# Four wide score products in a row, then four narrow corrections, in the recurrent layer of a two-layer backbone

## The chip, the cores and the metric

The kernel runs on one core of one Trainium2 chip. The metric is the device time of one execution in microseconds, as the median of several runs. All data is fp32 in DRAM; most matrix products split their operands into a rounded part and a remainder ("hi" and "lo") and add three products.

## The reference

A latent stream of 512 tokens by 1024 features and a context of 256 tokens pass through two layers. The first layer mixes the tokens with a bidirectional gated recurrence (8 heads of 128), the second with a short convolution; each is followed by a squared-ReLU MLP with 4096 hidden units. Norms are modulated by vectors from a conditioning input (adaLN). The part that matters here is one chunk of the recurrence, run for each head and direction:

```python
def step(s, blk):
    qb, kb, vb, gb = blk
    cum = jnp.cumsum(gb, axis=2)
    ref = cum[:, :, CHUNK // 2 - 1:CHUNK // 2]
    last = cum[:, :, -1:]
    o_inter = jnp.einsum('bhck,bhkv->bhcv', qb * jnp.exp(cum), s)
    scores = jnp.einsum('bhck,bhsk->bhcs', qb * jnp.exp(cum - ref), kb * jnp.exp(ref - cum))
    scores = jnp.where(lower, scores, 0.0)
    o_intra = jnp.einsum('bhcs,bhsv->bhcv', scores, vb)
    s_new = jnp.exp(last[:, :, 0, :, None]) * s + jnp.einsum(
        'bhsk,bhsv->bhkv', kb * jnp.exp(last - cum), vb)
    return s_new, o_inter + o_intra
```

Chunks are 64 tokens long. The output is the latent stream after a final norm.

## The kernel before

The program has three stretches: up to about 95 us the adaLN vectors, the norm and the first projections; from there to about 490 us the recurrent layer, head by head; behind it the MLPs and the convolution layer, which are long rows of 512-column products.

The recurrent layer works on pairs of heads. For each head TensorE makes the forget gates of the latent tokens (`ps_fl`) and of the context (`ps_fc`). ScalarE and VectorE turn them into logs, running sums and exponentials (`logs`, lines 646 to 712) and into scaled queries and keys (`latent_ops`, lines 740 to 761). Meanwhile TensorE makes the values (`psv`, even heads) or a gate projection (`ps_p`, odd heads). Then the recurrence of the head begins: `context_states` (line 714) transposes the context keys (`ctr`, written by VectorE at line 711) and makes the start states (`cst`), and `recurrence` (line 794) does both directions and the output.

The kernel takes two 64-token chunks together as one block of 128 tokens, so a head has four blocks `n`. In `scores` (line 763) a block's scores are one product of 128 by 128 (line 768, weights `kt`, moving `qt`). A 64 by 64 quarter of it, where queries of one chunk meet keys of the other, has the wrong scaling, and a second product from the sliced keys and queries `kl` and `ql` writes over that quarter (line 769). It lands on PSUM partitions 0 to 63 in the forward direction (`f` = 0) and 64 to 127 in the backward one. All four blocks of a direction lie in one PSUM tile `sc`; VectorE copies its unmasked entries out with one `copy_predicated` (line 772, `scm`).

Around it, for each direction, `states` (line 774) transposes scaled keys (`ktr`), which ScalarE copies (`kT`, line 781), makes the state products (`kv`, line 784) and lets VectorE update the states in three steps (`S`, line 789). When both directions are through, VectorE adds the two score tiles (`scs`, line 804) and TensorE makes the output `po` (lines 808 to 810; the third product of a block reads `scs`).

TensorE's order in a recurrence is written out by hand. Each of its instructions goes through `fill.step`, which chains it behind the last one, and `fill.gap` puts a number of product instructions of the next head (or of the output projection, `ps_woa`) in between; the numbers stand in the table `GAPS`. The PSUM tiles `ctr`, `cst`, `ktr`, `kv` and `sc` come from one pool of three buffers (`ps_sm`), so a new tile waits until VectorE or ScalarE has read an older one. VectorE's queue also holds the rounding remainders of weights (line 317) and sums for later adaLN vectors (`acc`, lines 442 and 444), which wait for their own DMAs.

Of the kernel before, what the change touches and what calls it, by code (L numbers as in the profile page):

```python
# [46 lines left out]
def dit_kernel(ctx, tc, x, c, ctx_in, c_ctx, ada_w, ada_b, norm1, norm2, norm_f, mlp_w1, mlp_w2,  # L47
# [28 lines left out]
    def sm_tile(name):  # L76
        return ps_sm.tile([P, 512], F32, tag="sm", name=name)
# [67 lines left out]
    for nm, ap in (("norm1", n1),  # L145
# [5 lines left out]
        n = ap.shape[0]  # L151
# [611 lines left out]
    def scores(o, d, hd, fill):  # L763
        ps = sm_tile(f"sc_{hd}_{d}")
        f = d
        for n in range(4):
            s = slice(n * P, (n + 1) * P)
            fill.step(nc.tensor.matmul(ps[:, s], lhsT=o["kt"][:, s], rhs=o["qt"][:, s], start=True, stop=True))  # L768
            fill.step(nc.tensor.matmul(ps[64 * f:64 * f + 64, n * P + 64 * (1 - f):n * P + 64 * (1 - f) + 64],
                                       lhsT=o["kl"][:, n * 64:n * 64 + 64], rhs=o["ql"][:, n * 64:n * 64 + 64],  # L770
                                       start=True, stop=True))
        nc.vector.copy_predicated(scm[d], pm[d], ps.rearrange("p (n t) -> p n t", t=P))
# [21 lines left out]
    def recurrence(hd, ops, s0, v, fill):  # L794

        S = []
        for d in range(2):
            S.append(states(ops[d], d, s0[d], v, f"{hd}_{d}", fill))
            if d:
                fill.gap()  # L800
            scores(ops[d], d, hd, fill)
# [457 lines left out]
```

## Time and profile before

| | before |
|---|---|
| median of 3 runs | 1429.88 us (1428.97 to 1430.18) |
| the profiled execution | 1430.36 us, its span 1428.6 us |
| TensorE, matmul | 1372.0 us busy, 96% |
| TensorE, weight loads | 1165.9 us busy, 82% |
| VectorE | 911.0 us, 64% |
| ScalarE | 578.6 us, 40% |
| mean granted TensorE clock | 0.990 |
| wide score products (line 768) | 128 instructions, first at 108.3, last at 476.8 us |
| corrections (line 769) | 128 instructions, first at 108.6, last at 477.1 us |

A busy TensorE is not TensorE at its peak: matmuls are pipelined, a recorded matmul is longer than its distance to the next one, and its end is modelled. The distance from start to start tells more. PE is the matmul row, PEld the weight load of the same instruction; 128\*64 is the part of the array that a matmul uses, rows by columns.

### The profile page before, as it was taken

The page shows a single profiled execution, that of the slowest core. Times are in us where ns is not written, and L with a number is a line of the kernel's source. Part 1 is how long each engine was busy: PE and PEld are TensorE (multiplying, and loading weights), DVE is VectorE, ACT ScalarE, POOL GpSimd, SP SyncE. Part 2 cuts the span into 40 slices and gives each one's busy share as a digit, 9 for nine tenths or more (in the row PEclk, how much of TensorE's full clock was granted, in tenths as well). Part 3 has the DMA queues.
Part 4 walks back from the last instruction along what each step waited for, and adds up shares of the span by engine and source line. Part 5 has one row for each costly group of instructions (what it writes and reads, how often), then busy time and mean ns, then how long its engine had stood idle before and what let it go on. Part 6 is the DMA issues. An engine that isn't in the chain of part 4 may idle for free.

```text
span 1428.6 us, 18668 instructions
## 1 busy us (share of the span) xinstructions
PE 1372.0 (96%) x7418; PEld 1165.9 (82%) x7418; DVE 911.0 (64%) x1378; ACT 578.6 (40%) x877; POOL 79.0 (6%) x87
## 2 busy tenths in 40 slices
PE   6999999999996989999999999999999999999997
PEld 4798887977885888888888889888889888888887
DVE  5695877878669598666576447544578544544536
ACT  6573447336435354133341433322244423142333
POOL 3000000000000121000000002000030100000000
PEclk9999999999998999999999999999999999999999
DMA  9713313423202235666555322332334533233311
GB/s 266 208 46 118 96 38 118 134 89 103 75 30 67 65 105 197 201 206 210 174 176 180 116 89 75 104 99 93 103 101 136 177 93 99 90 102 97 96 59 60
DMA packets 142267, 167.60 MB, mean 117 GB/s; under 512 B 6692, under 2 KB 121572, under 8 KB 142180
## 3 DMA queue, kind: packets, MB, share of 16 engines
q1 hardware_dynamic: 140964, 164.70, 36.4%
q0 software_dynamic: 1088, 1.65, 0.5%
q8 instruction: 58, 0.95, 0.3%
q14 instruction: 29, 0.24, 0.1%
q10 hardware_dynamic: 128, 0.05, 0.0%
HBM read 164.25 MB, written 2.14 MB: 116 GB/s over the span
## 4 chain that ended last, share of the span: by engine, by line
PE 74%; DVE 16%; DMA 3%; ACT 3%; issue 2%; SPq 0%; POOL 0%; DVEq 0%; ACTq 0%
PE ps_w L340 20%; PE ps_w L343 10%; PE ps_w2t L1197 4%; PE ps_w2t L1198 4%; PE ps_w2t L1196 4%; PE ps_fl L340 3%; DMA ada<-in_ada_w_dram 3%; PE ps_cvb L340 2%; PE ps_cwo L340 2%; PE ps_cvx L340 2%; PE ps_cvc L340 2%; PE ps_fl L343 2%; PE ps_fc L340 2%; PE sc L768 1%; PE ps_p L340 1%
## 5 line engine op out<-in xcount | busy, mean ns | idle before, releaser
L316 ACT CAST whi_w<-raw_w 128x1024 fp32r<-128x1024 f32 x128 | 134.0, 1051 | 277.0 <-PE ps_w L340 146.1
L317 DVE TENSOR_TENSOR wlo_w<-raw_w,whi_w 128x1024 fp32r<-128x1024 f32 x116 | 141.4, 1223 | 161.7 <-ACT whi_w L316 161.2
L340 PE MATMUL ps_w<-h_a_hi,whi_w 128*128 128x512 f32 (+1 forms) x576 | 207.6, 367 | 2.4 <-ACT h_a_hi L232 2.4
L340 PE MATMUL ps_w<-h_a_lo,whi_w 128*128 128x512 f32 x448 | 174.6, 390 | 0.0
L340 PEld LDWEIGHTS ps_w<-h_a_hi,whi_w 128*128 128x128 f32 x576 | 108.6, 189 | 21.1 <-ACT h_a_hi L232 2.8
L444 DVE SCALAR_TENSOR_TENSOR acc<-ada,cs,acc 128x1024 f32<-128x1024 f32 x70 | 89.8, 1282 | 50.8 <-DMA ada<-in_ada_w_dram 50.7
L343 PE MATMUL ps_w<-h_a_hi,wlo_w 128*128 128x512 f32 x448 | 119.8, 389 | 0.0
L1196 PE MATMUL ps_w2t<-whi_w,u_hi 128*128 128x512 f32 (+1 forms) x288 | 105.4, 366 | 0.0
L1197 PE MATMUL ps_w2t<-wlo_w,u_hi 128*128 128x512 f32 (+1 forms) x288 | 105.4, 366 | 0.0
L1198 PE MATMUL ps_w2t<-whi_w,u_lo 128*128 128x512 f32 (+1 forms) x288 | 105.4, 366 | 0.0
L340 PE MATMUL ps_w<-u_lo,whi_w 128*128 128x512 f32 (+1 forms) x288 | 103.4, 366 | 0.5 <-DVE u_lo L1068 0.5
L340 PE MATMUL ps_w<-u_hi,whi_w 128*128 128x512 f32 (+1 forms) x288 | 103.4, 366 | 0.0
L340 PEld LDWEIGHTS ps_w<-h_a_lo,whi_w 128*128 128x128 f32 x448 | 84.2, 188 | 17.4
L343 PEld LDWEIGHTS ps_w<-h_a_hi,wlo_w 128*128 128x128 f32 x448 | 84.1, 188 | 17.4
L1067 DVE TENSOR_TENSOR mr<-mr 128x512 f32<-128x512 f32 (+1 forms) x72 | 45.0, 630 | 46.2 <-ACT u_hi L1066 46.2
L1065 ACT ACTIVATE mr<-ps_w 128x512 f32<-128x512 f32 (+1 forms) x72 | 39.2, 544 | 81.0 <-PE ps_w L343 80.9
L343 PE MATMUL ps_w<-u_hi,wlo_w 128*128 128x512 f32 (+1 forms) x288 | 70.2, 366 | 0.0
L340 PEld LDWEIGHTS ps_w<-u_lo,whi_w 128*128 128x128 f32 x288 | 54.4, 189 | 9.8 <-DVE u_lo L1068 1.0
L340 PEld LDWEIGHTS ps_w<-u_hi,whi_w 128*128 128x128 f32 x288 | 54.3, 189 | 9.1
L1196 PEld LDWEIGHTS ps_w2t<-whi_w,u_hi 128*128 128x128 f32 x288 | 54.4, 189 | 8.8
L1198 PEld LDWEIGHTS ps_w2t<-whi_w,u_lo 128*128 128x128 f32 x288 | 54.4, 189 | 8.8
L1197 PEld LDWEIGHTS ps_w2t<-wlo_w,u_hi 128*128 128x128 f32 x288 | 54.4, 189 | 8.7
(374 smaller groups left out, 3124.0 us busy)
## 6 DMA issues: line engine op xcount, KB each, us to landing
raw_w<-in_mlp_w_dram SPq DMA_DIRECT2D x128, 512.0 KB, 3.7
ada<-in_ada_w_dram SPq DMA_DIRECT2D x80, 512.0 KB, 4.5
adaw<-in_ada_w_dram SPq DMA_DIRECT2D x32, 256.0 KB, 5.4
raw_f<-in_hgrn_w_in_dram SPq DMA_DIRECT2D x32, 256.0 KB, 3.9
raw_p<-in_hgrn_w_in_dram SPq DMA_DIRECT2D x12, 512.0 KB, 3.6
raw_v<-in_hgrn_w_in_dram SPq DMA_DIRECT2D x8, 512.0 KB, 4.2
raw_cvb<-in_conv_w_in_dram SPq DMA_DIRECT2D x8, 512.0 KB, 3.5
raw_cwo<-in_conv_w_out_dram SPq DMA_DIRECT2D x8, 512.0 KB, 3.4
```

Source lines behind the costliest of these rows:

```text
L316: pins[name] = nc.scalar.copy(hi, raw)
L317: eng.tensor_tensor(out=lo, in0=raw, in1=hi, op=ALU.subtract)
L340: yield nc.tensor.matmul(ps, lhsT=w[i][:, k % KH, ms], rhs=rhs[k][j][:, c0:c1], start=(k == first and (i, j) == (0, 0)), stop=False)
L343: yield nc.tensor.matmul(ps, lhsT=w[late[0]][:, k % KH, ms], rhs=rhs[k][late[1]][:, c0:c1], start=False, stop=(k == last))
L444: ins = nc.vector.scalar_tensor_tensor(out=acc, in0=raw[:, 0, :], scalar=cs[:, j, 0:1], in1=acc, op0=ALU.mult, op1=ALU.add)
L768: fill.step(nc.tensor.matmul(ps[:, s], lhsT=o["kt"][:, s], rhs=o["qt"][:, s], start=True, stop=True))
L1065: nc.scalar.activation(r, ps, AF.Relu)
L1067: nc.vector.tensor_tensor(out=r, in0=r, in1=r, op=ALU.mult)
L1196: nc.tensor.matmul(ps, lhsT=u[k][0][:, tk], rhs=whi[:, kk, c0:c1], start=(k == 0), stop=False)
L1197: nc.tensor.matmul(ps, lhsT=u[k][0][:, tk], rhs=wlo[:, kk, c0:c1], start=False, stop=False)
L1198: nc.tensor.matmul(ps, lhsT=u[k][1][:, tk], rhs=whi[:, kk, c0:c1], start=False, stop=(k == KT - 1))
```

## The change

The loop over the four blocks becomes two loops. The first issues the four 128-wide products, the second the four 64-wide corrections. Operands, targets and the number of instructions are the same.

```diff
         for n in range(4):
             s = slice(n * P, (n + 1) * P)
             fill.step(nc.tensor.matmul(ps[:, s], lhsT=o["kt"][:, s], rhs=o["qt"][:, s], start=True, stop=True))
+        for n in range(4):
             fill.step(nc.tensor.matmul(ps[64 * f:64 * f + 64, n * P + 64 * (1 - f):n * P + 64 * (1 - f) + 64],
                                        lhsT=o["kl"][:, n * 64:n * 64 + 64], rhs=o["ql"][:, n * 64:n * 64 + 64],
                                        start=True, stop=True))
```

TensorE's order in the forward direction of head 0, before (`kv` are the state products, `sc` the scores, `e` and `zb` the scaled queries and keys, `ktr` the transposes of the backward direction; in brackets what an instruction waits for):

```order
L784 MATMUL kv_0_1256<-vl_1049,kT_0_1254 128x128 x2
L768 MATMUL sc_0_1266<-e_0_0_982,zb_0_960 128x128 [waits DVE_49,PE_49]
L769 MATMUL sc_0_1266<-ql_0_1013,kl_0_1014 64x64 [waits DVE_49]
L768 MATMUL sc_0_1266<-e_0_0_982,zb_0_960 128x128
L769 MATMUL sc_0_1266<-ql_0_1013,kl_0_1014 64x64
L768 MATMUL sc_0_1266<-e_0_0_982,zb_0_960 128x128
L769 MATMUL sc_0_1266<-ql_0_1013,kl_0_1014 64x64
L768 MATMUL sc_0_1266<-e_0_0_982,zb_0_960 128x128
L769 MATMUL sc_0_1266<-ql_0_1013,kl_0_1014 64x64
L778 MATMUL ktr_1_1276<-ident,g_1_973 128x128 [waits DVE_49,PE_49]
```

The same place on TensorE with the change:

```order
L785 MATMUL kv_0_1256<-vl_1049,kT_0_1254 128x128 x2
L768 MATMUL sc_0_1266<-e_0_0_982,zb_0_960 128x128 [waits DVE_49,PE_49]
L768 MATMUL sc_0_1266<-e_0_0_982,zb_0_960 128x128 x3
L770 MATMUL sc_0_1266<-ql_0_1013,kl_0_1014 64x64 [waits DVE_49]
L770 MATMUL sc_0_1266<-ql_0_1013,kl_0_1014 64x64 x3
L779 MATMUL ktr_1_1276<-ident,g_1_973 128x128 [waits DVE_49,PE_49]
```

The three later wide products move ahead of all corrections, and the correction that waits for VectorE comes fifth instead of second. What follows the group is the same.

The backward direction of head 2 on TensorE, with the change (`ps_fl` are products for the next head):

```order
L343 MATMUL ps_fl_2054<-h_0_hi,wlo_f_0_2043 128x512
L768 MATMUL sc_1_2143<-e_2_1_1820,zb_1_1736 128x128 [waits DVE_49]
L768 MATMUL sc_1_2143<-e_2_1_1820,zb_1_1736 128x128 x3
L770 MATMUL sc_1_2143<-ql_1_1852,kl_1_1853 64x64 x4
L343 MATMUL ps_fl_2054<-h_1_hi,wlo_f_0_2043 128x512
```

The first wide product still holds the group's wait for VectorE, and the neighbours on both sides are those of before. All 16 groups change in this way; on the other engines and in the queues nothing moves.

## Rows read from the trace of the kernel before

**Rows 1.** The page, part 1: busy time, share of the span, instructions.

```profile
PE 1372.0 (96%) x7418; PEld 1165.9 (82%) x7418; DVE 911.0 (64%) x1378; ACT 578.6 (40%) x877; POOL 79.0 (6%) x87
```

**Rows 2.** Waits of TensorE, 95 to 490 us: us in total, times, longest.

```profile
PE ctr L718 <- DVE kc L711: 5.4, 3, 2.0
PE adaps L461 <- DVE alo L455: 2.9, 1, 2.9
```

**Rows 3.** TensorE in order of time, head 0: start, us, instruction, count, idle before.

```profile
107.66 0.83 PE L784 MATMUL kv<-vl,kT 128*128 128x128 f32 x6
108.33 0.39 PE L768 MATMUL sc<-e,zb 128*128 128x128 f32 x2
...
110.93 0.55 PE L778 MATMUL ktr<-ident,g 128*128 128x128 f32 x3
```

**Rows 4.** In order of time, 109.3 to 109.7 us: matmuls and weight loads.

```profile
109.11 0.28 PE L768 MATMUL sc<-e,zb 128*128 128x128 f32 x1
...
109.32 0.19 PEld L769 LDWEIGHTS sc<-ql,kl 128*64 128x64 f32 x2
109.32 0.33 PE L769 MATMUL sc<-ql,kl 128*64 128x64 f32 x2
109.58 0.30 PEld L768 LDWEIGHTS sc<-e,zb 128*128 128x128 f32 x2
```

**Rows 5.** Instructions of the tile sc: count, ns min/median/max, first and last start.

```profile
L769 PEld LDWEIGHTS sc<-ql,kl x128: 132/134/136, 108.6 to 477.1; 128*64 128x64 f32 x128
```

**Rows 6.** Waits of all engines, 95 to 490 us: us in total, times, longest.

```profile
DVE scm L772 <- PE sc L769: 12.6, 9, 2.3
...
DVE S L789 <- PE kv L784: 7.0, 6, 1.8
```

**Rows 7.** VectorE and TensorE in order of time, head 0, backward direction and output.

```profile
113.60 0.75 DVE L442 TENSOR_SCALAR acc<-ada,cs 128x1024 f32<-128x1024 f32 x1 [4.03 <-DMA ada<-in_ada_w_dram]
...
116.11 0.34 DVE L789 SCALAR_TENSOR_TENSOR S<-S,e,kv 128x128 f32<-128x128 f32 x1
...
116.50 0.49 PE L768 MATMUL sc<-e,zb 128*128 128x128 f32 x2 [1.82 <-DVE S L789]
...
123.02 0.69 DVE L804 TENSOR_TENSOR scs<-scm,scm 128x512 f32<-128x512 f32 x1
...
123.90 0.39 PE L810 MATMUL po<-scs,vl 128*128 128x128 f32 x2
```

**Rows 8.** VectorE and TensorE in order of time, head 2, backward direction.

```profile
203.08 0.72 DVE L772 COPY_PREDICATED scm<-mu,sc 128x512 f32<-128x512 uint8 x1
...
203.85 0.49 PE L768 MATMUL sc<-e,zb 128*128 128x128 f32 x2 [0.35 <-DVE scm L772]
```

**Rows 9.** The same in heads 3 and 6: third state update, backward group.

```profile
255.27 0.35 DVE L789 SCALAR_TENSOR_TENSOR S<-S,e,kv 128x128 f32<-128x128 f32 x1
...
256.53 0.38 PE L768 MATMUL sc<-e,zb 128*128 128x128 f32 x2
...
409.74 0.34 DVE L789 SCALAR_TENSOR_TENSOR S<-S,e,kv 128x128 f32<-128x128 f32 x1
...
410.56 0.38 PE L768 MATMUL sc<-e,zb 128*128 128x128 f32 x2
```

**Rows 10.** The same in head 1, and the second copy of head 4.

```profile
160.50 0.74 DVE L772 COPY_PREDICATED scm<-mu,sc 128x512 f32<-128x512 uint8 x1
...
162.80 0.38 PE L768 MATMUL sc<-e,zb 128*128 128x128 f32 x2
...
313.04 0.74 DVE L772 COPY_PREDICATED scm<-mu,sc 128x512 f32<-128x512 uint8 x1 [0.66 <-PE sc L769]
```

**Rows 11.** Stretches, heads 0 and 4: us, busy by engine, granted clock, DMA.

```profile
116.00:118.00 2.00, 1.50 (x9) 1.12 (x10) 1.31 (x4) 0.00 (x0) 0.00 (x0) 1.00 0.80 246
...
298.00:301.00 3.00, 1.06 (x5) 0.73 (x6) 2.97 (x5) 1.04 (x2) 0.10 (x1) 0.93 0.59 231
301.00:304.00 3.00, 3.00 (x9) 2.33 (x8) 2.65 (x4) 1.33 (x4) 0.51 (x1) 0.50 0.13 33
```

## The prediction

> **What bounds the kernel now.** I read the page first: TensorE is busy 96% of the span, VectorE 64% [rows 1]. The edited function runs only in the recurrent stage, about 95 to 490 us, so next come TensorE's own waits there. They are few: three on the context keys, 5.4 us together, one of 2.9 us on a row of adaLN values [rows 2], and short ones below. Wherever TensorE waits for nothing, a microsecond taken from its queue is a microsecond off the path, until another engine is late. Two questions are left: how many microseconds leave TensorE's queue, and how many VectorE gives back.
>
> For the first I read TensorE in order of time through one score group, head 0, forward direction [rows 3]. The six 128-wide state products before it start 0.112 us apart (107.66 to 108.33). The group takes 108.33 to 110.93, that is 2.60 us, for four wide products and four corrections. Each product is two matmul instructions: the tile has 128 instructions of each kind for 64 products [rows 5]. So eight wide instructions at 0.112 us would be 0.90 us of the 2.60. The rest sits at the changes of width, and a narrow window shows how [rows 4]. The second wide matmul starts at 109.11; the first narrow weight load does not start until 109.32, 0.21 us later, where 0.112 us would do, and the narrow matmul starts with its load instead of behind it. At the way back the next wide load starts at 109.58, 0.26 us after the first narrow load, again together with its matmul. Inside a pair this does not happen: two narrow loads, 0.132 us each [rows 5], end 0.19 us after the first began [rows 4], so the second starts 0.057 us after the first. What is lost is lost at each change of width, in both directions. The 15 other groups in the trace keep the same spacing.
>
> **The change, part by part.** It adds and removes no instruction and no transfer; on the other four engines the order stays. In each of 16 groups (8 heads, 2 directions) the changes of width fall from 8 to 2.
>
> *A group.* Before: 2.60 us from its first matmul to the first load behind it. After: seven steps of 0.112 us to the last wide matmul, 0.78; 0.21 to the first narrow load; 0.26 for the first pair up to the next wide load; six more narrow instructions. Their step in a run of eight is not in the trace. It lies between 0.057 us, load to load inside a pair, and 0.112 us, the wide step; a step below 0.057 I exclude, since two loads are seen no closer. I take 0.057, the row of the same instruction: 6 x 0.057 = 0.34. Sum 1.59, so 1.01 us saved; at 0.112 it is 0.67. Over 16 groups TensorE loses 16.2 us of work, or 10.8.
>
> *The wait that moves.* In the forward groups the first correction waits for its query slice. It now stands fifth instead of second, which can only help. Its copy on VectorE waits for the last instruction of the group, as it did.
>
> *What VectorE gives back.* Of a head's two savings, both come behind the wait for the context keys. Each must pass the point where the backward group gets its PSUM buffer, and then the product that needs the summed scores. Head by head, if VectorE keeps its times:
> - Head 0: the backward group already waits 1.82 us for a state update, which stands behind an adaLN sum that waited 4.03 us for its DMA [rows 7]. The first saving is eaten there. The second is eaten at the output product: its third pair starts at 123.90, the summed scores end at 123.02 + 0.69 = 123.71 and are held by the same DMAs. Kept: 0.1.
> - Heads 1, 5 and 7: the buffer is free long before. In head 1, the tightest of them, the copy ends at 161.24 and the group starts at 162.80 [rows 10]. Kept: 2.0 each.
> - Head 2: the group starts at 203.85, right at the end of the copy at 203.08 [rows 8]. The first saving is eaten, the second kept: 1.0.
> - Head 3: the third state update ends at 255.62 and the group would come at 255.52 [rows 9]. Kept: 1.9.
> - Head 4: the second copy waited 0.66 us for TensorE [rows 10]. It can move by that and by the 1.0 us by which the state updates ahead of it move, 1.66. The adaLN sums beside it read DMAs that need not move, so between 0.7 and 1.66; I take 1.4, nearer the end that the wait on TensorE supports.
> - Head 6: the last update ends at 410.08 and the group would come at 409.55 [rows 9]. Half a microsecond is lost: 1.5.
>
> Together 0.1 + 6.0 + 1.0 + 1.9 + 1.4 + 1.5 = 11.9 us; with the 0.67 us group 8.4. The chain of the next head starts from TensorE's products and a short piece on ScalarE, so what is kept at a head's end is passed on. Behind the stage the products follow one another and keep the shift.
>
> The profiled execution took 1430.36 us (span 1428.6). Less 11.9 it is 1418.5. The median of the runs, 1429.88, lies 0.5 lower than that execution, so the forecast is **1418.0 us**; with the dearer narrow step it is 1421.5.
>
> **The rivals.**
> *All of it is kept.* VectorE waited for the scores 9 times, 12.6 us in all, and for the state products 7.0 us [rows 6], so it too would start earlier; were the DMAs early as well, all 16.2 us come off: 1413.7. Against it stand the three heads whose group begins at VectorE's signal.
>
> *Narrow loads do not hide.* If a narrow load in the long run has to wait until the matmul before it has gone through, a step is 0.132 + 0.057 = 0.19 us, six of them 1.14 instead of 0.34, and a group saves 0.21. That is 3.4 us in TensorE's queue, and with the share kept above, 11.9 of 16.2, 2.5 us: 1427.4. For it: no run of more than two is in the trace. Against it: the second load of a pair begins while the first is still going, and the wide loads run ahead at 0.112 us a step [rows 3, 4]. The Trainium skill says on its page "TensorE: Matmul & The Clock Gate", section "Part 3: Packing small matmuls", that weight loads overlap running matmuls only where they use other rows of the array. All loads here use all 128 rows, so by that rule this rival would be the outcome; the spacing of 0.112 us in the trace speaks against it.
>
> *VectorE sets the pace everywhere.* Then each saving turns into a longer wait at the buffer or the output product, as in head 0, and about 1.5 us is left: 1428.4. For it: in heads 2 and 6 the copies and updates of VectorE come just in time [rows 8, 9]. Against it: the 19.6 us that VectorE spent waiting for these very products [rows 6].
>
> *Slower: the clock falls.* After the 2.9 us wait, in head 4 [rows 2], the granted clock was 0.93 and then 0.50, that is 1.2 GHz, for 3 us [rows 11]: 0.07 x 3 + 0.50 x 3 = 1.7 us lost. The change lengthens waits: head 0's from 1.82 to 2.8, head 2's from 0.35 to 1.36. It decides if waits between 1.8 and 2.8 us bring the clock down: behind the 1.82 us of head 0 it stood at 1.00, 2.4 GHz [rows 11]. If six more heads lost it at half clock, 10.2 us, and VectorE left only 6 us of the savings, the kernel would take 4.2 us more: 1434.1. One fall, in head 0, costs 1.7 and belongs to the forecast's own range.
>
> That the change doesn't do what it says is excluded: TensorE's order shows the runs of four.
>
> **How the numbers follow.** A difference under 0.2%, 2.9 us, is what a measurement of this kernel can't tell from none. Chances: the forecast 0.77 (its own range 1414.5 to 1423.5), all kept 0.10, loads that do not hide 0.05, VectorE's pace 0.05, clock 0.03. The first two are faster, 0.87; the next two are within 0.2%, 0.10; the last is slower, 0.03. The range goes down to 1413.0, past the case in which all is kept, and up to 1424.0: the dearer narrow step, 1421.5, with head 0's fall of the clock, 1.7, and head 4 at its lower end, 0.7. What it leaves out are the last three rivals, 0.13, and the edges of the first two.
>
> **What would show it right or wrong.** Right: a score group that lasts 1.6 us instead of 2.60, with wide matmuls 0.112 us apart, narrow loads 0.057 us apart, one gap of 0.2 us between them; a wait of some 2.8 us ahead of head 0's backward group, 1.4 in head 2, 0.5 in head 6; a wait of 0.9 us at head 0's output product; all work after 490 us unchanged and about 12 us earlier. A narrow step near 0.19 us proves the second rival, a group of 1.6 us with long waits in odd heads the third, a granted clock of 0.50 in the recurrences the fourth. The forecast's mechanism is wrong if the gaps stay between the narrow matmuls themselves.

## The result, and the profile after

The changed kernel takes 1420.87 us (median of 9 runs, 1414.42 to 1425.73); the kernel before, timed beside it, takes 1431.87 us (9 runs, 1428.97 to 1435.67). The medians lie 11.0 us apart. The ratio is 0.9913 with a 95% interval of 0.9895 to 0.9931; of 1431.87 us that is 12.5 us. The profiled execution took 1422.73 us, its span 1420.8 us, at a mean granted clock of 0.985; the profiled execution of before had 0.990.

The page, part 1, for the changed kernel: busy time, share and instructions of each engine.

```profile
PE 1361.4 (96%) x7418; PEld 1162.3 (82%) x7418; DVE 910.9 (64%) x1378; ACT 578.7 (41%) x877; POOL 78.9 (6%) x87
```

The counts are those of [rows 1], and VectorE has the same work. TensorE is busy 10.6 us less, and its share of the span has not moved.

TensorE in order of time, head 0, forward direction: start, us, instruction, count.

```profile
107.59 0.83 PE L785 MATMUL kv<-vl,kT 128*128 128x128 f32 x6
108.25 1.06 PE L768 MATMUL sc<-e,zb 128*128 128x128 f32 x8
109.24 0.68 PE L770 MATMUL sc<-ql,kl 128*64 128x64 f32 x8
109.85 0.55 PE L779 MATMUL ktr<-ident,g 128*128 128x128 f32 x3
```

The group goes from 108.25 to 109.85, 1.60 us; it was 2.60 [rows 3]. The weight loads of the corrections, in the same view, tell the step in the long run:

```profile
109.24 0.54 PEld L770 LDWEIGHTS sc<-ql,kl 128*64 128x64 f32 x8
```

Eight loads take 0.54 us from the first start to the last end. How long one lasts is told by the instructions of the tile `sc` (count, ns min/median/max, first and last start):

```profile
L770 PEld LDWEIGHTS sc<-ql,kl x128: 132/138/231, 109.2 to 469.7; 128*64 128x64 f32 x128
```

One load lasts 0.138 us in the middle, a little more than in [rows 5], so seven steps fill 0.40 us: 0.057 us each.

What TensorE waits for, 90 to 485 us: us in total, times, longest.

```profile
PE ps_woa L343 <- DVE y_lo L230: 12.4, 1, 12.4
PE ctr L718 <- DVE kc L711: 5.4, 3, 2.0
PE sc L768 <- DVE S L790: 4.3, 2, 4.0
PE adaps L461 <- DVE alo L455: 3.1, 1, 3.1
PE sc L768 <- DVE scm L773: 1.0, 1, 1.0
```

The wait for the context keys is that of [rows 2], the one for the adaLN row 0.2 us longer, and the 12.4 us ahead of 447 us stood in this view of before too, with the same number. The two waits of `sc` are those that the change moved. In order of time, the backward groups of heads 0, 2 and 6 (and head 0's corrections):

```profile
117.61 2.07 PE L768 MATMUL sc<-e,zb 128*128 128x128 f32 x8 [4.01 <-DVE S L790]
119.61 1.12 PE L770 MATMUL sc<-ql,kl 128*64 128x64 f32 x8
...
204.00 1.16 PE L768 MATMUL sc<-e,zb 128*128 128x128 f32 x8 [1.04 <-DVE scm L773]
...
404.80 1.16 PE L768 MATMUL sc<-e,zb 128*128 128x128 f32 x8 [0.28 <-DVE S L790]
```

Head 0 waits 4.01 us where it waited 1.82 [rows 7], and its eight wide instructions last 2.07 us where head 2's last 1.16. VectorE there, in order of time:

```profile
113.18 0.75 DVE L442 TENSOR_SCALAR acc<-ada,cs 128x1024 f32<-128x1024 f32 x1 [3.69 <-DMA ada<-in_ada_w_dram]
...
116.01 1.28 DVE L444 SCALAR_TENSOR_TENSOR acc<-ada,cs,acc 128x1024 f32<-128x1024 f32 x1 [1.44 <-DMA ada<-in_ada_w_dram]
117.21 0.34 DVE L790 SCALAR_TENSOR_TENSOR S<-S,e,kv 128x128 f32<-128x128 f32 x1
```

The third state update, which frees the buffer, comes at 117.21; before it came at 116.11. It stands behind two adaLN sums that wait for their DMAs. The clock in that stretch (us, busy PE, PEld, DVE, ACT, POOL, then granted clock, DMA share, GB/s):

```profile
114.00:117.00 3.00, 0.00 (x0) 0.00 (x0) 1.53 (x3) 0.00 (x0) 0.00 (x0) 0.79 0.63 201
117.00:120.00 3.00, 2.39 (x12) 2.17 (x13) 2.65 (x6) 0.00 (x0) 0.00 (x0) 0.50 0.55 187
120.00:123.00 3.00, 3.00 (x13) 2.44 (x13) 2.69 (x6) 0.00 (x0) 0.00 (x0) 0.57 0.00 0
```

It fell to 0.50, 1.2 GHz, during the wait and stayed low for the group and the work behind it. In [rows 11] it was 1.00 in the same place.

So that two executions can be followed beside one another, this table takes the start of a head's first output product (`po`) and gives how many us earlier it starts than in the profiled execution of before (123.46 in head 0, 481.52 in head 7). The last row is the end of the span. The columns behind the changed kernel are two more executions of it and three other kernels of the section below.

| head | changed | again | third | unchanged | backward | forward |
|---|---|---|---|---|---|---|
| 0 | -2.31 | 0.00 | -1.07 | -2.34 | 1.73 | -1.34 |
| 1 | -0.26 | 2.05 | 0.98 | -2.33 | 2.40 | -1.91 |
| 2 | 0.86 | 3.07 | 1.99 | -2.22 | 3.40 | -3.34 |
| 3 | 2.61 | 4.84 | 3.76 | -2.20 | 4.44 | -2.59 |
| 4 | 3.27 | 8.51 | 7.24 | -2.09 | 5.26 | -1.51 |
| 5 | 5.33 | 12.10 | 10.86 | -0.50 | 7.78 | 1.10 |
| 6 | 6.67 | 13.43 | 12.19 | -0.66 | 8.79 | 1.41 |
| 7 | 7.40 | 15.66 | 14.32 | -0.97 | 9.31 | 1.85 |
| end | 7.8 | 12.6 | 12.3 | -2.7 | 7.0 | -2.5 |

### The profile page after: what moved, and what is told of

Its sections match the earlier page's. It is cut to its first block, busy times and chain, and to the rows that moved or that the text cites. A ratio compares the mean times of both kernels' runs of the same rounds, so it can differ in the third digit from the quotient of the medians.

```text
span 1420.8 us, 18668 instructions
## 1 busy us (share of the span) xinstructions
PE 1361.4 (96%) x7418; PEld 1162.3 (82%) x7418; DVE 910.9 (64%) x1378; ACT 578.7 (41%) x877; POOL 78.9 (6%) x87
## 4 chain that ended last, share of the span: by engine, by line
PE 76%; DVE 16%; DMA 3%; ACT 2%; issue 2%; SPq 0%; POOL 0%; DVEq 0%; ACTq 0%
PE ps_w L340 22%; PE ps_w L343 11%; PE ps_w2t L1199 4%; PE ps_w2t L1197 4%; PE ps_w2t L1198 4%; PE ps_fl L340 2%; DMA ada<-in_ada_w_dram 2%; PE ps_cvb L340 2%; PE ps_cwo L340 2%; PE ps_cvx L340 2%; PE ps_cvc L340 2%; PE ps_fc L340 1%; PE ps_p L340 1%; PE ps_fl L343 1%; PE ps_cvb L343 1%
```

## The experiments

Two theories were on trial. The first: time is lost only where the width of the weights changes, so a group's length follows from the number of changes. The second: TensorE's queue keeps what it saves, except where VectorE or a DMA is late, and the clock may take some of it back when it falls, that is, when the granted clock goes from 1.00 to 0.50 for a few us.

All runs in one table. "Lost" is worked out from the stretches view: over all stretches of 3 us, one minus the granted clock, times TensorE's busy time, summed. It estimates how much shorter the execution would be at 2.4 GHz throughout; the next column is span minus lost. The two executions of the kernel before lie 2.3 us apart in it, so smaller differences tell nothing. The kernel before, timed beside them, took 1431.87 us (changed), 1433.78 (again, head0, retuned, backward), 1431.75 (pairs, forward, lagged, wide) and 1431.25 (forward_rest, unchanged, retuned_again, third).

| run | median us | ratio (95%) | span | lost | span less lost |
|---|---|---|---|---|---|
| before | 1431.87 | | 1428.6 | 6.6 | 1422.0 |
| unchanged | 1433.32, one run | | 1431.3 | 11.6 | 1419.7 |
| changed | 1420.87 | 0.9913 (0.9895 to 0.9931) | 1420.8 | 11.7 | 1409.1 |
| again | 1418.78 | 0.9891 (0.9869 to 0.9914) | 1416.0 | 8.1 | 1407.9 |
| third | 1419.06 | 0.9911 (0.9888 to 0.9934) | 1416.3 | 6.4 | 1409.9 |
| head0 | 1418.78 | 0.9894 (0.9868 to 0.9921) | 1417.9 | 9.7 | 1408.2 |
| retuned | 1416.95 | 0.9880 (0.9856 to 0.9904) | 1417.2 | 10.0 | 1407.2 |
| retuned_again | 1419.92 | 0.9914 (0.9892 to 0.9935) | 1419.8 | 11.7 | 1408.1 |
| backward | 1425.41 | 0.9944 (0.9924 to 0.9964) | 1421.6 | 7.4 | 1414.2 |
| forward | 1432.74 | 1.0000 (0.9988 to 1.0013) | 1431.1 | 17.1 | 1414.0 |
| forward_rest | 1429.40 | 0.9987 (0.9970 to 1.0004) | 1426.7 | 12.0 | 1414.7 |
| pairs | 1424.82 | 0.9949 (0.9929 to 0.9969) | 1425.0 | 15.3 | 1409.7 |
| lagged | 1431.49, one run | | 1429.5 | 13.6 | 1415.9 |
| wide | 1424.86, one run | | 1422.9 | 12.9 | 1410.0 |

### What a change of width costs: pairs, lagged, wide

**pairs**, against the changed kernel: two wide products, two corrections, and the same once more.

```diff
-        for n in range(4):
...
-        for n in range(4):
...
+        size = 2
+        for n0 in range(0, 4, size):
+            for n in range(n0, n0 + size):
...
+            for n in range(n0, n0 + size):
...
```

> The changed order with runs of two: two wide products, two corrections, and once more. A group has four changes of width, where the kernel before has eight and the changed kernel two. If the loss sits at each change of width, and a pair of changes costs what the two kernels show, (2.60 - 1.60) / 3 = 0.33 us, a group lasts 2.60 - 2 x 0.33 = 1.93 us, and the queue loses 16 x 0.67 = 10.7 us, of which about two thirds should be kept: 7 us off the kernel before. Rival: the loss comes from going back to a wide product right behind a correction of the block just written, and a run of any length over one removes it: the group would last 1.6 us as in the changed kernel.

TensorE in order of time, head 0, forward direction:

```profile
106.54 0.61 PE L770 MATMUL sc<-e,zb 128*128 128x128 f32 x4
107.08 0.45 PE L772 MATMUL sc<-ql,kl 128*64 128x64 f32 x4
107.46 0.71 PE L770 MATMUL sc<-e,zb 128*128 128x128 f32 x4
108.10 0.45 PE L772 MATMUL sc<-ql,kl 128*64 128x64 f32 x4
108.47 0.33 PE L781 MATMUL ktr<-ident,g 128*128 128x128 f32 x1
```

106.54 to 108.47 is 1.93 us, the number expected. The rival, 1.6 us for any run over one, is out. The time fell by 6.9 us, where 7 was expected, but that agreement is luck in part. By the starts inside heads 1 to 7 pairs keeps 8.9 us, more than the two thirds that were assumed; in its profiled execution the clock lost 15.3 us, and by the last column it would be 11.2 us below the kernel before.

**lagged**, against the kernel before: the alternating order, but a correction comes one wide product later.

```diff
-        for n in range(4):
...
+        for i in range(5):
+            if i < 4:
+                s = slice(i * P, (i + 1) * P)
...
+            n = i - 1
+            if n < 0:
+                continue
```

> The alternating order, but each correction comes one wide product later, so that it never writes into the block that the product ahead of it has just written: wide 0, wide 1, correction 0, wide 2, correction 1, wide 3, corrections 2 and 3. It has six changes of width. If the loss is the change of width, it costs 0.33 us for each pair of changes: the group lasts 2.60 - 0.33 = 2.27 us, with the gaps of 0.2 us at every change. Rival: the gap is a wait for the block just written: then no gap is left and the group lasts 1.4 us or less.

The same view, from the first wide product to the work behind the group:

```profile
107.85 0.61 PE L769 MATMUL sc<-e,zb 128*128 128x128 f32 x4
108.39 0.33 PE L773 MATMUL sc<-ql,kl 128*64 128x64 f32 x2
108.65 0.49 PE L769 MATMUL sc<-e,zb 128*128 128x128 f32 x2
...
109.74 0.45 PE L773 MATMUL sc<-ql,kl 128*64 128x64 f32 x4
110.12 0.33 PE L782 MATMUL ktr<-ident,g 128*128 128x128 f32 x1
```

2.27 us, again the number expected, although no correction writes into the block just written. The way back to a wide product takes 0.26 us (108.39 to 108.65) as in [rows 4]. The time of its one run is that of the kernel before; by the last column, with 13.6 us lost, it would be 5.0 us lower.

**wide**, against the kernel before: the alternating order, the corrections with 128 weight columns (the last block uses its neighbour's columns as well). Such a correction also overwrites the other half of its 64 columns, so a part of the scores is changed.

```diff
-            fill.step(nc.tensor.matmul(ps[64 * f:64 * f + 64, n * P + 64 * (1 - f):n * P + 64 * (1 - f) + 64],
-                                       lhsT=o["kl"][:, n * 64:n * 64 + 64], rhs=o["ql"][:, n * 64:n * 64 + 64],
+            fill.step(nc.tensor.matmul(ps[:, n * P + 64 * (1 - f):n * P + 64 * (1 - f) + 64],
+                                       lhsT=o["kl"][:, min(n, 2) * 64:min(n, 2) * 64 + 128], rhs=o["ql"][:, n * 64:n * 64 + 64],
```

> The alternating order with corrections whose weights are 128 columns wide instead of 64, so that all products write all 128 partitions; a correction then also overwrites half a block that it should leave, so that a part of the scores is changed. Nothing changes width any more. If the loss is the change of width, the gaps of 0.2 us vanish and the group lasts 4 x (2 x 0.112 + 2 x 0.06 to 0.112) = 1.4 to 1.8 us although the order alternates. Rival: the loss comes from alternating long and short products, or from writing a block twice in a row: the group stays near 2.6 us.

The same view, the first three steps, the last and the work behind:

```profile
107.58 0.39 PE L768 MATMUL sc<-e,zb 128*128 128x128 f32 x2
107.81 0.33 PE L769 MATMUL sc<-ql,kl 128*128 128x64 f32 x2
107.98 0.44 PE L768 MATMUL sc<-e,zb 128*128 128x128 f32 x2
...
109.15 0.33 PE L769 MATMUL sc<-ql,kl 128*128 128x64 f32 x2
109.32 0.28 PE L778 MATMUL ktr<-ident,g 128*128 128x128 f32 x1
```

The group takes 1.74 us in the alternating order. Its weight loads, in the same window:

```profile
107.47 0.30 PEld L768 LDWEIGHTS sc<-e,zb 128*128 128x128 f32 x2
107.70 0.30 PEld L769 LDWEIGHTS sc<-ql,kl 128*128 128x128 f32 x2
107.92 0.30 PEld L768 LDWEIGHTS sc<-e,zb 128*128 128x128 f32 x2
```

Two loads of either kind take 0.22 us to the next two, the 0.112 us of a wide step, so neither the alternation nor the overwriting leaves a gap. What costs is the change of the weights' width (with it goes the number of PSUM partitions written, 64 or 128; these runs can't part the two). The four kernels with 8, 6, 4 and 2 changes (2.60, 2.27, 1.93, 1.60 us) lie on one line: a pair of changes costs 0.33 us.

The Trainium skill says on its page "TensorEngine Tiling (Array Packing)", section "Tiling Modes", under "Key Properties", that changing the tiling mode, and not just the tile, drains TensorE. The traces agree: 128 by 64 beside 128 by 128 is such a change. The page gives no price; here it is the 0.33 us for there and back.

### Which half keeps what: backward, forward

**backward** and **forward** have rows of four in one direction only, and alternate in the other (against the changed kernel).

```diff
-        for n in range(4):
...
-        for n in range(4):
...
+        size = 4 if d == 1 else 1
+        for n0 in range(0, 4, size):
+            for n in range(n0, n0 + size):
...
+            for n in range(n0, n0 + size):
...
```

(`d == 0` in forward.)

> Only the backward groups have the rows of four, the forward ones alternate. By the reading that the forward saving is eaten in heads 0 and 2 and kept elsewhere (1.0 in heads 1, 5 and 7, 0.9 in head 3, 0.4 to 0.7 in head 4, 0.5 in head 6), 5 us of the gain go, and head 0 is spared its long wait, 2 us back: 3 us slower than the change, about 1424 us. In the trace, TensorE's shift against the kernel before grows by 1.0 us per head at the backward group in heads 1 to 7. Rival: VectorE sets the pace, and a saving ahead of the backward group is worth nothing in any head; then the time is that of the change or better.

Backward came out 8.0 us below the kernel before, by the ratio, and 6.6 above again, where 3 was expected. By the last column it is 5.2 us above the changed kernel, the 5 us that the forward savings were taken for; that the 2 us of head 0 do not show is left open. Inside each head from 1 on, TensorE gains 0.94 to 1.02 us between the start of the backward group and the output product, 7.0 us in all. Between the heads the table moves by the clock too (1.58 us more ahead of head 5, because a fall at 342 us is missing). Inside heads 1 to 7 nothing of a backward saving is lost.

> Only the forward groups have their products in runs of four; the backward groups alternate as before. Together with the run in which only the backward groups were changed this splits the saving. The theory says that a forward saving is kept where the PSUM buffer of the backward group is free in time (heads 1, 3, 4, 5 and 7, about 1.0 us each, 0.5 in head 6) and eaten in heads 0 and 2: 5.5 us off the kernel before. Rival: VectorE takes the forward savings back in all heads, since the whole saving of the backward run was already about half of the changed kernel's: then under 1.5 us off.

Forward came out level with the kernel before. That is the rival's number, but not its reason: VectorE does not hold the savings back. Its forward groups take 1.60 us (106.32 to 107.92 in head 0). From the start of the forward group to that of the backward one it gains 1.02, 0.85, 1.00, 1.01, 0.42 and 1.01 us in heads 1, 3, 4, 5, 6 and 7: 5.3 us, where the theory had 5.5. Less what the clock took its span is 1414.0 us, 6.9 below the mean of the two executions of the kernel before (1420.9) and as low as backward's. The clock took the saving: 17.1 us are lost, against 6.6 and 11.6. In the starts 3.0 us go in head 0 and 1.5 in head 2, both between the backward group and the output product, and 4.3 more behind head 7. The mean clock of all its timed executions says the same: median 0.984 in 12, where the kernel before, beside it, had 0.990 in 17. What that is worth can be read from those 17: the five at 0.986 or 0.987 took 1435.2 us on the mean, the other twelve 1431.3. The largest loss begins in head 0, behind a longer wait; TensorE in order of time:

```profile
114.86 0.49 PE L770 MATMUL sc<-e,zb 128*128 128x128 f32 x2 [3.19 <-DVE S L792]
```

And the stretches behind it:

```profile
114.00:117.00 3.00, 2.14 (x10) 1.51 (x10) 1.67 (x4) 0.00 (x0) 0.00 (x0) 0.84 0.73 224
117.00:120.00 3.00, 3.00 (x10) 2.25 (x10) 2.68 (x4) 0.00 (x0) 0.00 (x0) 0.50 0.26 105
120.00:123.00 3.00, 3.00 (x9) 2.35 (x8) 1.65 (x4) 0.00 (x0) 0.00 (x0) 0.52 0.00 0
```

**forward_rest** is forward with head 0 left alternating.

```diff
-        size = 4 if d == 0 else 1
+        size = 4 if d == 0 and hd > 0 else 1
```

> Rows of four in the forward groups of heads 1 to 7 only; head 0 and all backward groups alternate. With head 0's forward group in rows of four the run before this one came out no faster: its profile has a wait of 3.19 us ahead of head 0's backward group and the clock at half speed behind it, and more such falls later. Theory: the clock took the saving, and the wait in head 0 began it. Then here the wait is 1.8 us again, the clock from 114 to 123 us stays at 1.00, and at least the 3.3 us lost in head 0 come back: 3 to 5 us off the kernel before. Rival: forward savings do not last whatever head 0 does, as other waits behind them (head 2's, head 6's, the context keys') bring the clock down instead: within 1.5 us of the kernel before.

1.85 us off, between the two expectations, and its interval reaches from 0.6 us above to 4.3 below, so the time decides nothing. The step in head 0 holds: the wait is 1.49 us and the clock behind it 1.00. TensorE in order of time, heads 0 and 2, backward groups:

```profile
114.74 0.49 PE L770 MATMUL sc<-e,zb 128*128 128x128 f32 x2 [1.49 <-DVE S L792]
...
201.05 0.49 PE L770 MATMUL sc<-e,zb 128*128 128x128 f32 x2 [1.36 <-DVE scm L775]
```

The stretches, heads 0 and 2:

```profile
117.00:120.00 3.00, 3.00 (x15) 2.38 (x15) 2.79 (x4) 0.00 (x0) 0.00 (x0) 1.00 0.26 102
...
201.00:204.00 3.00, 2.95 (x17) 2.18 (x18) 1.29 (x5) 0.00 (x0) 0.00 (x0) 0.94 0.00 0
204.00:207.00 3.00, 3.00 (x8) 2.32 (x9) 1.31 (x2) 0.00 (x0) 0.00 (x0) 0.50 0.00 0
```

But the rest of the theory was too simple. As in forward, the clock falls in head 2, behind a wait of 1.36 us (1.06 in forward), and 1.5 us go there. Another 4.5 us go behind the stage (6.42 us ahead at head 7's output product, 1.95 at the end), where this execution has falls near 504, 567 and 1065 us, at none of which the profiled execution of before has one.

In head 2 the executions with rows of four behind a wait of 1.04 to 1.4 us (changed, again, third, head0) keep 1.00, and so does wide, with 1.29 us and an alternating group without gaps. There, only a wait with a group full of gaps behind it was followed by a fall, in both cases that there are. In head 0 the same pattern was followed by none: the waits of 1.49 us here, 1.82 in before and 1.90 in head0 have an alternating group behind them and the clock stays at 1.00. So it is not shown that a row of four in the backward group protects the clock, and why forward loses most to it stays open. Inside the heads the two halves do add up: 7.0 us in backward and 5.3 in forward, against 12.2 in heads 1 to 7 of again.

### Head 0 and the clock: head0, unchanged, again, third

**head0** is the changed kernel with head 0's groups alternating.

```diff
-        for n in range(4):
...
+        size = 1 if hd == 0 else 4
+        for n0 in range(0, 4, size):
+            for n in range(n0, n0 + size):
...
```

> Head 0 keeps the alternating order, heads 1 to 7 have the rows of four. If the longer wait in head 0 brings the clock down and costs what the trace of the change shows (its output product 2.3 us later than before), this kernel is 2 us faster than the changed one, near 1418.5, the group of head 0 takes 2.6 us, the wait ahead of the backward group is near 1.8 us, and the clock stays at 1.00 from 116 to 122 us. Rival: the state update itself came late through its DMA, whatever the score groups do; then the wait is again near 3 to 4 us less the 1 us of the alternating group, the clock falls too, and the time is that of the change.

The wait is 1.90 us and the clock in head 0 stays at 1.00; at head 0's output product its trace is 2.29 us ahead of again's. The medians are equal all the same, and so are the medians of the mean clock, 0.989: in the profiled executions head0 has falls at 21, 296 and 335 us, again in their place at 116, 495 and 874. The step works in the trace, and the time does not show it.

> The changed kernel as it is, once more, to see what its own runs differ in. My reading: its times spread because head 0's backward group waits about 4 us for a state update that stands behind an adaLN sum and its DMA, and the clock falls to 1.2 GHz there in some executions and not in others. Then executions with a mean clock near 0.985 take about 1422 us, those near 0.990 about 1416, and a profile with the higher clock shows a wait of 3 us or less at that place and no fall. Rival: the spread comes from other places (DMA, the end of the kernel); then head 0 looks the same at both mean clocks.

Again's wait is 2.81 us, as the prediction had it, but the reading fails: at a mean clock of 0.989 the clock went to 0.59 behind that wait all the same, and third, at 0.990, shows it too. The rival, other places, is right for the larger part. The first profiled execution, at 0.985, has falls near 297 and 342 us that again and third don't have, and by the table it loses 3.0 us between heads 3 and 4 and 1.5 between heads 4 and 5 against again; from head 0's start to its output product the difference is 1.9. Again's ratio agrees with the changed kernel's within the intervals.

**unchanged** is the kernel before, profiled a second time.

> The kernel before, unchanged, profiled again beside the others. The theory that a wait of about 2.8 us ahead of head 0's backward group brings the clock down and one of 1.8 us does not expects 1.8 us here and a clock of 1.00 from 114 to 123 us. The rival, that the clock falls by chance or by the chip, would show a fall there. It also tells how many of the falls at other places (21, 153, 207, 300, 345, 501, 882, 1062 us) the kernel before has in a second execution.

The expectation fails in an instructive way: this execution of the kernel before has a wait of 2.64 us and a fall. TensorE in order of time, head 0:

```profile
115.80 0.49 PE L768 MATMUL sc<-e,zb 128*128 128x128 f32 x2 [2.64 <-DVE S L789]
```

The stretches there:

```profile
114.00:117.00 3.00, 1.20 (x7) 0.89 (x8) 2.61 (x5) 0.00 (x0) 0.00 (x0) 1.00 0.71 193
117.00:120.00 3.00, 3.00 (x12) 2.26 (x13) 2.03 (x3) 0.00 (x0) 0.00 (x0) 0.60 0.52 165
120.00:123.00 3.00, 3.00 (x8) 2.33 (x8) 2.39 (x4) 0.00 (x0) 0.00 (x0) 0.50 0.00 0
```

TensorE reached head 0 1.5 us earlier than in the first execution, and the state update, held by the adaLN DMAs, came only 0.7 us earlier (115.41 against 116.11). The rest became wait, and the fall cost 3.0 us by the output product (0.70 ahead to 2.34 behind). So the wait is set by when TensorE and the DMAs happen to arrive, in both kernels, and the change adds its 1.0 us to it.

> The changed kernel unchanged for a third time, beside the retuned one. Expected is 11 to 15 us off the kernel before, a wait of 2.8 us or more ahead of head 0's backward group, and the clock at 0.50 behind it. A clock of 1.00 behind such a wait would speak against the theory.

The third execution of the changed kernel, TensorE in order of time, head 0:

```profile
117.08 1.88 PE L768 MATMUL sc<-e,zb 128*128 128x128 f32 x8 [2.88 <-DVE S L790]
```

The eight wide instructions last 1.88 us, so the clock fell within the group (0.55 from 117 to 120 us); the time, 12.2 us off, is as expected. Over all 14 profiled executions the waits ahead of head 0's backward group were 0.72, 1.39, 1.49, 1.78, 1.82, 1.90 us with the clock at 1.00 behind the group, and 2.64, 2.81, 2.88, 3.06, 3.15, 3.19, 3.36, 4.01 us with a fall. No execution breaks the order.

### Filling the waits: retuned

Other numbers in the gap table of the changed kernel put more products of the next head ahead of the backward groups of heads 0, 2 and 6, and fewer behind them.

```diff
-GAPS = ((0, 9, 4, 6, 5, 18, 9),
+GAPS = ((0, 9, 4, 6, 14, 9, 9),
...
-        (0, 9, 4, 6, 2, 12, 12),
+        (0, 9, 4, 6, 6, 8, 12),
...
-        (0, 9, 4, 6, 2, 12, 12),
+        (0, 9, 4, 6, 4, 10, 12),
```

> The change, with filling products of the next head moved from behind the backward score group to ahead of it: nine in head 0, four in head 2, two in head 6; nothing is added. If TensorE's waits there are only waits, the arrival at the output product does not move and head 2 and head 6 give the same times as the change; but head 0's wait shrinks from 4.0 to about 2 us, the clock stays at 1.00, and 2 to 3 us come off: about 1418.5 us, with less spread than the change. If the clock is not what costs time in head 0, the time is that of the change.

> The changed kernel with the gap table that puts more of the other work ahead of the backward groups of heads 0, 2 and 6, for a second time. The first time it was 1.8 us faster than the changed kernel beside it, with intervals that overlap. If its gain is real, it is 1.5 to 3 us below the changed kernel again, with head 0's wait under 1 us and the clock there at 1.00; if not, the two medians lie within 1 us of one another.

The wait in head 0 shrank to 0.72 and 1.39 us and the clock held at the group, but the time is the changed kernel's: 1.8 us below it the first time, 0.9 above it the second, with overlapping intervals. There was little to win: from head 0's start to its last output product again and third lose 0.5 us against the kernel before, and retuned none. The filling left waits at head 0's output product, and in the second execution the clock fell there, to 0.50 from 123 to 129 us. TensorE in order of time:

```profile
121.75 0.49 PE L810 MATMUL po<-c,S 128*128 128x128 f32 x2 [1.65 <-DVE S L790]
123.11 0.80 PE L811 MATMUL po<-scs,vl 128*128 128x128 f32 x2 [0.88 <-DVE scs L805]
```

No version is shown to beat the changed kernel.

## Why the prediction was right, and where it was not

**The group.** 1.59 us was worked out, 1.60 measured. The one term that was not in the trace, the narrow step in a long run, was taken as 0.057 us and measured the same. With that the rival of narrow loads that do not hide (0.19 us a step) is dead. The rule of the Trainium skill's page "TensorE: Matmul & The Clock Gate", section "Part 3: Packing small matmuls", by which loads overlap matmuls only on other rows of the array, is not what these records show: all loads use all 128 rows and the corrections' follow one another at 0.057 us, while a correction's matmul is recorded with 0.222 us (its end is modelled).

**What VectorE gives back.** At full clock the changed kernel's three executions have 1409.1, 1407.9 and 1409.9 us, mean 1409.0, against 1420.9 for the two of the kernel before: 11.9 us, the forecast's sum. The two of before lie 2.3 us apart, so the exact agreement is luck, and head 4's 0.6 us more makes up for heads 0, 3 and 6. By heads, from the table and the starts inside a head, without the clock:

- Heads 1, 5 and 7: 2.05, 2.0 and 2.04 us kept, 2.0 forecast.
- Head 2: 1.33, 1.02 and 1.01 in the three executions, 1.0 forecast; its wait is 1.04 to 1.4 us, 1.4 forecast.
- Head 3: 1.75 to 1.77, 1.9 forecast. Head 6: 1.3 to 1.5, 1.5 forecast; its wait is 0.28 to 0.4 us, 0.5 forecast.
- Head 4: 2.0, 1.4 forecast. The guess between 0.7 and 1.66 was too careful. In again the copy starts 1.1 us earlier after the head's start than before; the rest comes out of slack that the forecast left out: the summed scores were ready 1.17 us ahead of the product that reads them (315.54 to 316.71 in before), and now are 0.22 us ahead.

"All kept" is out by heads 0, 2, 3 and 6, and "VectorE sets the pace" by the rest. VectorE has less slack left, though: its waits for the scores fell from 12.6 us [rows 6] to 3.0 (all engines, 90 to 490 us):

```profile
DVE scm L773 <- PE sc L770: 3.0, 5, 1.3
```

**Head 0** is the step that failed. The forecast was a wait of 2.8 us, 0.1 us kept and one fall of the clock, for 1.7 us, as a matter of the range. The wait was 4.01, 2.81 and 2.88 us, and the clock fell in all three executions. From the head's start to its output product they lost 2.4, 0.5 and 0.5 us. In the first, 1.1 us of it is the state update that came later with its DMAs. The wait of 0.9 us at the output product did not come in any of them: its pairs start 0.22 us apart as before. The slow clock brought TensorE there later than the summed scores (in again they are done at 123.29 us and the third pair starts at 123.90). In backward, where the clock stayed at 1.00, TensorE gains 1.02 us up to the output product and gives back 0.34 at its third pair. The forecast held VectorE and its DMAs at the times of one execution; unchanged shows that they move by as much as the term.

**The clock** as a rival was given 0.03, with falls in six more heads. It did not come in the changed kernel, whose losses (11.7, 8.1, 6.4 us) lie about where the two executions of before lie (6.6, 11.6). It did come in forward, where it ate the whole saving, so the mechanism is real. What spared the changed kernel is not shown: that its backward groups have no gaps fits head 2 and does not fit head 0.

**Behind the stage.** The forecast had everything after 490 us about 12 us earlier and unchanged. At 481 us the three executions are 7.4, 15.7 and 14.3 us ahead and at the end 7.8, 12.6 and 12.3. What again loses there, 3.1 us, is about the two falls near 495 and 1058 us, of 1.6 to 1.7 us each, that the first execution of before does not have; third has the one at 496. This fits the forecast that the products keep the shift, but for such falls.

**The total.** 1418.0 us forecast, 1420.87, 1418.78 and 1419.06 measured; all three lie in the range, and in the forecast's own case. The forecast was counted from 1429.88 us; timed beside the three, the kernel before took 1431.87, 1433.78 and 1431.25. Between the medians the saving was 11.0, 15.0 and 12.2 us, where 11.9 was forecast.

## What to carry to other kernels

Matmuls whose weights differ in width should be issued in runs of one width: here each pair of changes cost 0.33 us of TensorE's queue, and the order was free. Read the price from starts, not from busy time, and cost a saving head by head against the signal that releases the next tile. Where a saving turns into a wait, look at the granted clock behind it in several executions: of this change one half alone came out at nothing and the other at 8 us, with the same work saved on TensorE.

## What the runs showed of the hardware

By the stretches a fall of the clock costs 1.2 to 1.7 us of TensorE's work, the longer ones 2.5 to 3.4. In all 14 executions it falls at the wait of 12.4 us around 440 us (1.8 to 3.4 us). The other places recur from kernel to kernel (about 21, 114, 153, 300, 342, 500, 880 and 1062 us; near 207 in two executions, 567 in three), but at each the clock falls in some executions and not in others: head 1's wait of 2.03 to 2.05 us for the context keys was followed by one in 5 of 14, head 4's wait of 2.8 to 3.2 us for the adaLN row in 10 of 14, and the four without a fall (2.76 to 2.97 us) lie among the ten (2.78 to 3.21). So the length of a wait orders the falls ahead of head 0's backward group, and not there. Two executions of the same kernel differ by several us for this, and a single profile tells the clock's share poorly: the first execution of before lost 6.6 us, the second 11.6.
